# Block norms from channel-major squares, and h of two blocks kept in SBUF

## The chip, the cores and the metric

One core of a Trainium2 chip runs the kernel. The metric is device time in microseconds of one launch, the median of a few runs. The trace is of one further, profiled execution.

## The reference

One layer of a decoder: a pre-norm, one wide input projection, two mixers side by side, one output projection, a post-norm and the residual. What the change touches is the norm, the projection behind it, and the last columns of that projection (`dt_raw`).

```python
def rms_norm(x, w):
    xf = x.astype(jnp.float32)
    y = xf * lax.rsqrt(jnp.mean(xf * xf, axis=-1, keepdims=True) + EPS)
    return (y * w.astype(jnp.float32)).astype(x.dtype)

    h = rms_norm(x, pre_w)                       # x: (1, 2048, 1024)
    proj = jnp.einsum('bld,dc->blc', h, w_in)
    u, v, zg, z, xbc, dt_raw = jnp.split(proj, SPLITS, axis=-1)
    ...
    dt = jax.nn.softplus(dt_raw.astype(f32) + dt_bias.astype(f32))
    ...
    mixed = jnp.einsum('blc,cd->bld', jnp.concatenate([y_a, y_b], axis=-1), w_out)
    return x + rms_norm(mixed, post_w)
```

## The kernel before

The 2048 tokens are four blocks of 512. The 1024 input channels are eight k-tiles of 128, taken as four pairs. `x` comes token-major (`x`) and channel-major (`x_t`).

**Products.** The big projections run as sums of seven products, P1 to P7, of sums and differences of operands, for two pairs of blocks, (0, 2) and (1, 3). Every operand is split into a high and a low part: ScalarE copies (`split`, L160), VectorE subtracts (L161); three wide matmuls of 128x512 follow (`mm3`, L165 to L167, into `acc`). Such a wide matmul is called a wide product below. A step is 24 of them. There are seven units of output columns, 28 steps in each of the first six and 56 in the last. In unit 0, steps 0 to 3 are P1 and P2 of the first pair, which need block 0 alone; steps 4 to 7 are those of the second pair, which need block 1; steps 8 to 11 are P6 and P7 of the first pair (blocks 0 and 2), steps 12 to 15 those of the second (blocks 1 and 3). A product's finished sum is copied out of PSUM by ScalarE (`p` for P1, `stage` for P2). Sums have five PSUM banks.

**`prep(b)`**, once for each block: loads eight tiles of `x` by tokens (`load_x`, L239), squares and sums them on ScalarE (L184), makes `x_ms` (L171, VectorE) and the reciprocal root `x_r` (L173, a power on GpSimd), puts it on a diagonal `dg` (L254, VectorE), and spreads it over partitions on TensorE (`r_ps`, L259; copied to `rb`, L261). It then loads `x_t` in four pieces (L265), scales them in place by the norm's weight and `rb` (L268, eight operations on VectorE), stores them to `hd` in HBM (L269), and computes `dt_ps`, 32 small matmuls of 128x16 on TensorE (L273; each has two records in the trace). `make_a` loads the operands of P1 to P7 from `hd` again (L153).

**Order.** Each engine takes its instructions in a fixed order, and so does SP, which issues nearly all DMAs. `prep` and other side work are tasks that are advanced between wide products; the numbers given to `spawn` and `yield` say how much later a task goes on:

```python
    spawn(prep(0))
    spawn(setup())
    spawn(prep(1), 1)
    spawn(prep(2), 16)
    spawn(prep(3), 30)
```

`setup` loads constants and has one GpSimd product over `wsT` (L129). A load from `w_u` brings weights; `a<-as0P...` (L736) loads a split operand that unit 0 stored, for use in later units. Tiles come from pools: `rt` takes one of 7 (128x1024), `gt` one of 32 (128x512).

Of the kernel before, what the change touches and what calls it, by code (L numbers as in the profile page):

```python
# [15 lines left out]
P = 128  # L16
# [35 lines left out]
def hybrid_kernel(ctx: ExitStack, tc: tile.TileContext, x, x_t, pre_w, w_u, w_o, w_dt,  # L52
# [15 lines left out]
    def bank(name):  # L68
        return ps.tile([P, T], F32, name=name, tag="ps")
# [4 lines left out]
    def gt(name):  # L74
        return gfull(name)[:, 0:T]
# [4 lines left out]
    def rt(name):  # L80
        return rpool.tile([P, 2, T], F32, name=name, tag="r")
# [94 lines left out]
    def rsqrt_mean2(ss, n, inv, name):  # L176
        tot = sm.tile([P, n], F32, name=name + "_tot")
        nc.vector.tensor_tensor(tot, ss[:, :, 0], ss[:, :, 1], ALU.add)
        return rsqrt_mean(tot, n, inv, name)
# [3 lines left out]
    def sumsq(dst, src, n):  # L183
        nc.scalar.activation(junk[:, 0:n], src, AF.Square, accum_out=dst)  # L184
# [17 lines left out]
    def spawn(gen, delay=0):  # L202
        task = [now[0] + delay, gen]
        tasks.append(task)
        if delay == 0:
            advance(task)
        return task
# [24 lines left out]
                then()  # L232


    def load_x(b):
        for c in range(NT):
            for n in range(2):
                xt = gt("xt")
                nc.sync.dma_start(out=xt, in_=x[(b * NT + c) * P:(b * NT + c + 1) * P, n * WC:(n + 1) * WC])  # L239
                yield c, n, xt  # L240

    def prep(b):

        ss = sm.tile([P, NT, 2], F32, name="x_ss")
        dg = gt("dg").rearrange("p (c n) -> p c n", c=NT)
        for c, n, xt in load_x(b):
            sumsq(ss[:, c, n:n + 1], xt, WC)
        if b == 0:
            for i, v in enumerate((dt_bias, a_log, d_skip)):
                nc.sync.dma_start(out=hvec[:, i, :], in_=v.partition_broadcast(P))  # L250
            nc.scalar.activation(na, hvec[:, 1, :], AF.Exp)
            nc.vector.tensor_scalar(na, na, -1.0, None, ALU.mult)
        r = rsqrt_mean2(ss, NT, 1.0 / DM, "x")
        nc.vector.tensor_tensor(dg, ident[:, :].unsqueeze(1).broadcast_to([P, NT, P]),  # L254
                                r[:, :].unsqueeze(2).broadcast_to([P, NT, P]), ALU.mult)
        if b:
            yield 0
        rp = bank("r_ps")
        nc.tensor.matmul(rp, lhsT=ones, rhs=dg.rearrange("p c n -> p (c n)"), start=True, stop=True)  # L259
        rb = gt("rb")  # L260
        nc.vector.tensor_copy(rb, rp)  # L261
        dtp = bank("dt_ps")
        for j in range(4):
            h = rt("h")
            nc.sync.dma_start(out=h, in_=x_t[b, j])  # L265
            for kk in range(2):
                k = 2 * j + kk
                nc.vector.scalar_tensor_tensor(h[:, kk, :], h[:, kk, :], pre_c[:, k:k + 1], rb, ALU.mult, ALU.mult)  # L268
            nc.sync.dma_start(out=hd[b][j], in_=h)  # L269
            for kk in range(2):  # L270
                k = 2 * j + kk
                for c in range(NT):
                    nc.tensor.matmul(dtp[:, c * NH:(c + 1) * NH], lhsT=h[:, kk, c * P:(c + 1) * P], rhs=wdt[:, k, :],  # L273
                                     start=k == 0 and c == 0, stop=k == KT - 1 and c == NT - 1, skip_group_check=True)
            if b:
                yield 0
        d = sm.tile([P, NG, NT, HG], F32, name=f"dt{b}", bufs=1)
        bias = hvec[:, 0, :].rearrange("p (g h) -> p g h", g=NG)
        for c in range(NT):
            nc.vector.tensor_tensor(d[:, :, c, :], dtp[:, c * NH:(c + 1) * NH].rearrange("p (g h) -> p g h", g=NG),  # L280
                                    bias, ALU.add)
        spawn(dt_chain(b, d), 20)
# [429 lines left out]
    def a_piece(u, p, m, k, j):  # L712
        b = PAIRS[p][m]
        if u < 6:
            return hd[b][2 * k + j]
        assert all((b, (0 if k else 4) + j, i) in y_in for i in range(2))
        return y_d[b][(0 if k else 4) + j]
# [3 lines left out]
    def make_a(u, p, name, j):  # L721

        piece = lambda m, k: a_piece(u, p, m, k, j)
        tt = nc.vector.tensor_tensor
        if name in PLAIN_A and not 1 < u < 6:
            t, = load([piece(*PLAIN_A[name])])
            yield
            w = split(apool, "a", t)
            if u == 1:
                store(a_d[p][name, j], w[:, :, :, :].bitcast(F32))  # L730
            yield w
            return
        if 0 < u < 6:
            yield
            w = apool.tile([P, 2, 2, T], F32R, name="a")
            nc.sync.dma_start(out=w[:, :, :, :].bitcast(F32), in_=a_d[p][name, j][:, :, :, :])  # L736
            yield w
            return
        if u == 0:
            yield  # L740
        if name == "P6":
            if u == 0:
                t, q, r = load([piece(0, 0), piece(1, 0), piece(1, 1)])
                tt(t, t, q, ALU.subtract)
                s3_in[p, j] = t
                tt(r, r, t, ALU.subtract)
                s2 = s2_in[p, j] = [gt("s2") for _ in range(2)]
                for kk in range(2):
                    nc.gpsimd.tensor_copy(s2[kk], r[:, kk, :])
                t = r  # L750
            else:
                q, t = load([piece(1, 1), s_d[p, "S3", j]])
                yield
                tt(t, q, t, ALU.subtract)
                store(s_d[p, "S2", j], t)
        elif name == "P7":
            if u == 0:
                t = s3_in.pop((p, j))
            else:
                t, q = load([piece(0, 0), piece(1, 0)])  # L760
                yield
                tt(t, t, q, ALU.subtract)
                store(s_d[p, "S3", j], t)
        elif name == "P5":
            t, q = load([piece(1, 0), piece(1, 1)])
            if u:
                yield
            tt(t, t, q, ALU.add)
        elif u == 0:
            t, = load([piece(0, 1)])  # L770
            s2 = s2_in.pop((p, j))
            for kk in range(2):
                tt(t[:, kk, :], t[:, kk, :], s2[kk], ALU.subtract)
        else:
            t, q = load([piece(0, 1), s_d[p, "S2", j]])
            yield
            tt(t, t, q, ALU.subtract)
        w = split(apool, "a", t)
        if u == 0:
            store(a_d[p][name, j], w[:, :, :, :].bitcast(F32))  # L780
        yield w
# [128 lines left out]

    nc.sync.dma_start(out=pre_c, in_=pre_w)
    nc.sync.dma_start(out=wdt, in_=w_dt)
    spawn(prep(0))
    spawn(setup())
    spawn(prep(1), 1)
    spawn(prep(2), 16)
    spawn(prep(3), 30)

    LAST = 3
    groups = [[i] for i in range(len(steps) - LAST)] + [list(range(len(steps) - LAST, len(steps)))]  # L920
# [86 lines left out]
```

## Time and profile before

| | us |
|---|---|
| median of 3 runs | 1588.78 (1585.33 to 1590.7) |
| the profiled execution | 1584.35 |
| its span | 1582.6 |
| TensorE busy in the span | 1508.9 (95%) |
| VectorE busy | 1068.9 (68%) |
| ScalarE busy | 819.8 (52%) |
| GpSimd busy | 390.1 (25%) |

The span is what the trace covers; the execution has 1.75 us around it. The engines work side by side, so their busy times add up to more than the span. The kernel moves 494.63 MB by DMA. The granted clock of TensorE, averaged over the span, is 0.979 of full speed.

### The profile page before, as it was taken

The page shows a single profiled execution, that of the slowest core. Times are in us where ns is not written, and L with a number is a line of the kernel's source. Part 1 is how long each engine was busy: PE and PEld are TensorE (multiplying, and loading weights), DVE is VectorE, ACT ScalarE, POOL GpSimd, SP SyncE. Part 2 cuts the span into 40 slices and gives each one's busy share as a digit, 9 for nine tenths or more (in the row PEclk, how much of TensorE's full clock was granted, in tenths as well). Part 3 has the DMA queues.
Part 4 walks back from the last instruction along what each step waited for, and adds up shares of the span by engine and source line. Part 5 has one row for each costly group of instructions (what it writes and reads, how often), then busy time and mean ns, then how long its engine had stood idle before and what let it go on. Part 6 is the DMA issues. An engine that isn't in the chain of part 4 may idle for free.

```text
span 1582.6 us, 21521 instructions
## 1 busy us (share of the span) xinstructions
PE 1508.9 (95%) x7268; PEld 1258.4 (80%) x7268; DVE 1068.9 (68%) x1708; ACT 819.8 (52%) x1769; POOL 390.1 (25%) x449
## 2 busy tenths in 40 slices
PE   4979999899999999999999999989999999999996
PEld 3868887788888888888778888867888878888775
DVE  3476874678665576567786768764665646587698
ACT  4432324655676545654466666859737742333332
POOL 1000000234232333342234515353523300000022
PEclk9988999999999999999999999989999999999999
DMA  9799999999998799986998788866776598897998
GB/s 333 264 371 357 338 411 397 392 340 366 374 349 311 240 353 341 329 316 238 333 338 319 271 299 275 279 229 225 276 252 242 193 302 326 275 384 239 341 351 333
DMA packets 160847, 494.63 MB, mean 313 GB/s; under 512 B 19040, under 2 KB 35808, under 8 KB 140768
## 3 DMA queue, kind: packets, MB, share of 16 engines
q1 hardware_dynamic: 160736, 493.25, 85.9%
q8 instruction: 57, 0.93, 0.2%
q14 instruction: 54, 0.44, 0.1%
HBM read 373.51 MB, written 119.67 MB: 312 GB/s over the span
## 4 chain that ended last, share of the span: by engine, by line
PE 57%; DMA 13%; DVE 11%; ACT 7%; issue 3%; POOL 1%; SPq 1%; DVEq 0%; ACTq 0%; POOLq 0%
PE acc L165 16%; PE acc L167 16%; PE acc L166 16%; DMA E<-scr 3%; DMA r<-yd 3%; PE y_ps L448 3%; ACT E L389 2%; DMA r<-w_o 2%; PE y_ps L451 1%; PE st_ps L453 1%; DVE cv_out L372 1%; DVE a L161 1%; PE s_ps L594 1%; PE y_tp L553 1%; DVE b L161 1%
## 5 line engine op out<-in xcount | busy, mean ns | idle before, releaser
L165 PE MATMUL acc<-b,a 128*128 128x512 f32 x1344 | 544.6, 406 | 16.1 <-DMA a<-as0P 5.4
L166 PE MATMUL acc<-b,a 128*128 128x512 f32 x1344 | 527.3, 392 | 0.0
L167 PE MATMUL acc<-b,a 128*128 128x512 f32 x1344 | 520.2, 393 | 4.3 <-DVE a L161 4.3
L165 PEld LDWEIGHTS acc<-b,a 128*128 128x128 f32 x1344 | 253.7, 189 | 71.3 <-DMA a<-as0P 5.6
L167 PEld LDWEIGHTS acc<-b,a 128*128 128x128 f32 x1344 | 253.2, 188 | 60.2 <-DVE a L161 6.3
L166 PEld LDWEIGHTS acc<-b,a 128*128 128x128 f32 x1344 | 254.0, 189 | 49.3
L160 ACT ACTIVATE a<-r 128x1024 fp32r<-128x1024 f32 x96 | 101.1, 1057 | 200.8 <-PE acc L167 88.5
L165 PE MATMUL acc<-a,b 128*128 128x512 f32 x448 | 182.4, 414 | 8.3 <-ACT b L160 4.2
L372 DVE SCALAR_TENSOR_TENSOR cv_out<-cv_raw,cw,cv_out 128x512 f32<-128x512 f32 x192 | 155.1, 810 | 41.5 <-ACT cv_out L370 39.5
L161 DVE TENSOR_TENSOR b<-r,b 128x1024 fp32r<-128x1024 f32 x112 | 141.9, 1270 | 60.6 <-ACT b L160 60.4
L166 PE MATMUL acc<-a,b 128*128 128x512 f32 x448 | 180.3, 403 | 0.8 <-DVE a L161 0.8
L167 PE MATMUL acc<-a,b 128*128 128x512 f32 x448 | 177.7, 400 | 0.0
L160 ACT ACTIVATE b<-r 128x1024 fp32r<-128x1024 f32 x112 | 117.2, 1052 | 86.9 <-PE acc L167 33.1
L161 DVE TENSOR_TENSOR a<-r,a 128x1024 fp32r<-128x1024 f32 x96 | 117.3, 1223 | 50.5 <-ACT a L160 50.3
L165 PEld LDWEIGHTS acc<-a,b 128*128 128x128 f32 x448 | 87.2, 195 | 27.4 <-ACT b L160 4.3
L184 ACT ACTIVATE junk<-y 128x128 bf16<-128x128 f32 (+1 forms) x192 | 65.5, 341 | 83.1 <-POOL y L465 71.4
L457 POOL TENSOR_TENSOR state<-state,ex 128x256 f32<-128x256 f32 x60 | 46.9, 781 | 239.5 <-PE y_ps L451 239.4
L166 PEld LDWEIGHTS acc<-a,b 128*128 128x128 f32 x448 | 86.8, 194 | 19.6 <-DVE a L161 1.8
L167 PEld LDWEIGHTS acc<-a,b 128*128 128x128 f32 x448 | 86.4, 193 | 18.9 <-issue 0.2
L436 POOL TENSOR_TENSOR xde<-xtok,dte 128x256 f32<-128x256 f32 x64 | 52.3, 824 | 165.0 <-ACT xtok L408 158.7
L173 POOL TENSOR_TENSOR o_r<-o_ms,mhalf 128x1 f32<-128x1 f32 x16 | 19.0, 1198 | 295.1 <-DVE o_ms L171 285.0
L389 ACT ACTIVATE E<-E,cs 128x128 f32<-128x128 f32 x256 | 79.6, 390 | 22.2 <-DMA E<-scr 22.2
(163 smaller groups left out, 2125.8 us busy)
## 6 DMA issues: line engine op xcount, KB each, us to landing
a<-as0P SPq DMA_DIRECT2D x64, 1024.0 KB, 7.4
a<-as1P SPq DMA_DIRECT2D x64, 1024.0 KB, 6.2
r<-w_u SPq DMA_DIRECT2D x108, 512.0 KB, 6.4
r<-yd SPq DMA_DIRECT2D x72, 512.0 KB, 5.3
r<-hd SPq DMA_DIRECT2D x48, 512.0 KB, 7.5
r<-w_o SPq DMA_DIRECT2D x36, 512.0 KB, 5.2
E<-scr SPq DMA_DIRECT2D x64, 256.0 KB, 7.4
yd<-yT SPq DMA_DIRECT2D x64, 256.0 KB, 4.4
```

Source lines behind the costliest of these rows:

```text
L160: nc.scalar.activation(w[:, :, 0, :], t, AF.Copy)
L161: nc.vector.tensor_tensor(w[:, :, 1, :], t, w[:, :, 0, :], ALU.subtract)
L165: nc.tensor.matmul(dst, lhsT=a_hi, rhs=b_hi, start=first, stop=False, skip_group_check=True)
L166: nc.tensor.matmul(dst, lhsT=a_hi, rhs=b_lo, start=False, stop=False, skip_group_check=True)
L167: return nc.tensor.matmul(dst, lhsT=a_lo, rhs=b_hi, start=False, stop=last, skip_group_check=True)
L173: nc.gpsimd.tensor_tensor(r, ms, mhalf[:, 0:n], ALU.pow)
L184: nc.scalar.activation(junk[:, 0:n], src, AF.Square, accum_out=dst)
L372: nc.vector.scalar_tensor_tensor(cv, raw[:, j:j + T], cw[:, ti, j:j + 1], cv, ALU.mult, ALU.add)
L389: nc.scalar.activation(E[:, h, :], E[:, h, :], AF.Relu, scale=-1.0, bias=dts[self.b]["cs"][:, o + h:o + h + 1])
L436: nc.gpsimd.tensor_tensor(h4(xde[:, :]), xc, hv(d["dte"], g, c), ALU.mult)
L448: nc.tensor.matmul(yps[:, h * HD:(h + 1) * HD], lhsT=E[:, h, :], rhs=xdt[:, h * HD:(h + 1) * HD], start=True, stop=True)
L457: nc.gpsimd.tensor_tensor(h4(st[:, :]), h4(st[:, :]), ev(d["ex"], 1, g, c), ALU.mult)
```

## The change

`prep` no longer loads `x` by tokens. It loads `x_t` alone, as eight halves of 128x512, and squares those on ScalarE (L257, L260 of the changed kernel). The eight squares are added up by VectorE for block 0, by GpSimd for blocks 1 to 3 (L261). Four TensorE matmuls with a vector of ones (`ss_ps`, L266, 128x2 each) finish the sum over partitions. The rest of the chain is as before (`x_ms`, `x_r`, `dg` L270, `r_ps` L278, `rb` L280). The halves are scaled in place (L285), stored to `hd` by halves (L286), and `dt_ps` is computed from them (L293). The scaled halves of blocks 0 and 1 stay in SBUF (`kept`), and `make_a` splits them from there for P1 and P2 of unit 0 (L754 ScalarE, L755 VectorE) instead of loading from `hd`. The tasks start at other points: `prep(1)` at once, `setup` later, `prep(2)` and `prep(3)` earlier; and a block's `prep` is driven forward when an operand asks for it.

```diff
--- before.py
+++ after.py
@@ -232,45 +232,65 @@
                 then()
 
 
-    def load_x(b):
-        for c in range(NT):
-            for n in range(2):
-                xt = gt("xt")
-                nc.sync.dma_start(out=xt, in_=x[(b * NT + c) * P:(b * NT + c + 1) * P, n * WC:(n + 1) * WC])
-                yield c, n, xt
+    kept, h_in = {}, set()
 
     def prep(b):
 
-        ss = sm.tile([P, NT, 2], F32, name="x_ss")
-        dg = gt("dg").rearrange("p (c n) -> p c n", c=NT)
-        for c, n, xt in load_x(b):
-            sumsq(ss[:, c, n:n + 1], xt, WC)
+
+        xs = []
+        for j in range(4):
+            if b:
+                halves = [gt("x") for _ in range(2)]
+            else:
+                t = rt("x")
+                halves = [t[:, kk, :] for kk in range(2)]
+            for kk in range(2):
+                nc.sync.dma_start(out=halves[kk], in_=x_t[b, j, :, kk, :])
+            xs += halves
         if b == 0:
             for i, v in enumerate((dt_bias, a_log, d_skip)):
                 nc.sync.dma_start(out=hvec[:, i, :], in_=v.partition_broadcast(P))
-            nc.scalar.activation(na, hvec[:, 1, :], AF.Exp)
-            nc.vector.tensor_scalar(na, na, -1.0, None, ALU.mult)
-        r = rsqrt_mean2(ss, NT, 1.0 / DM, "x")
+        else:
+            yield 4
+
+        total = gt("sq")
+        nc.scalar.activation(total, xs[0], AF.Square)
+        for k in range(1, KT):
+            sq = gt("sq")
+            nc.scalar.activation(sq, xs[k], AF.Square)
+            (nc.gpsimd if b else nc.vector).tensor_tensor(total, total, sq, ALU.add)
+        if b:
+            yield 9
+        ssp = bank("ss_ps")
+        for c in range(NT):
+            nc.tensor.matmul(ssp[:, 2 * c:2 * c + 2], lhsT=total[:, c * P:(c + 1) * P], rhs=ones[:, 0:2],
+                             start=True, stop=True)
+        r = rsqrt_mean(ssp[:, 0:2 * NT].rearrange("p (c i) -> p c i", i=2)[:, :, 0], NT, 1.0 / DM, "x")
+        dg = gt("dg").rearrange("p (c n) -> p c n", c=NT)
         nc.vector.tensor_tensor(dg, ident[:, :].unsqueeze(1).broadcast_to([P, NT, P]),
                                 r[:, :].unsqueeze(2).broadcast_to([P, NT, P]), ALU.mult)
         if b:
             yield 0
+        else:
+            nc.scalar.activation(na, hvec[:, 1, :], AF.Exp)
+            nc.vector.tensor_scalar(na, na, -1.0, None, ALU.mult)
         rp = bank("r_ps")
         nc.tensor.matmul(rp, lhsT=ones, rhs=dg.rearrange("p c n -> p (c n)"), start=True, stop=True)
         rb = gt("rb")
         nc.vector.tensor_copy(rb, rp)
         dtp = bank("dt_ps")
         for j in range(4):
-            h = rt("h")
-            nc.sync.dma_start(out=h, in_=x_t[b, j])
             for kk in range(2):
                 k = 2 * j + kk
-                nc.vector.scalar_tensor_tensor(h[:, kk, :], h[:, kk, :], pre_c[:, k:k + 1], rb, ALU.mult, ALU.mult)
-            nc.sync.dma_start(out=hd[b][j], in_=h)
+                nc.vector.scalar_tensor_tensor(xs[k], xs[k], pre_c[:, k:k + 1], rb, ALU.mult, ALU.mult)
+                nc.sync.dma_start(out=hd[b][j][:, kk, :], in_=xs[k])
+            h_in.add((b, j))
+            if b < 2:
+                kept[b, j] = xs[2 * j:2 * j + 2]
             for kk in range(2):
                 k = 2 * j + kk
                 for c in range(NT):
-                    nc.tensor.matmul(dtp[:, c * NH:(c + 1) * NH], lhsT=h[:, kk, c * P:(c + 1) * P], rhs=wdt[:, k, :],
+                    nc.tensor.matmul(dtp[:, c * NH:(c + 1) * NH], lhsT=xs[k][:, c * P:(c + 1) * P], rhs=wdt[:, k, :],
                                      start=k == 0 and c == 0, stop=k == KT - 1 and c == NT - 1, skip_group_check=True)
             if b:
                 yield 0
@@ -712,6 +732,8 @@
     def a_piece(u, p, m, k, j):
         b = PAIRS[p][m]
         if u < 6:
+            while (b, 2 * k + j) not in h_in:
+                advance(preps[b])
             return hd[b][2 * k + j]
         assert all((b, (0 if k else 4) + j, i) in y_in for i in range(2))
         return y_d[b][(0 if k else 4) + j]
@@ -722,6 +744,17 @@
 
         piece = lambda m, k: a_piece(u, p, m, k, j)
         tt = nc.vector.tensor_tensor
+        if u == 0 and name in ("P1", "P2"):
+            yield
+            b, i = PAIRS[p][0], 2 * PLAIN_A[name][1] + j
+            while (b, i) not in kept:
+                advance(preps[b])
+            w = apool.tile([P, 2, 2, T], F32R, name="a")
+            for kk, h in enumerate(kept.pop((b, i))):
+                nc.scalar.activation(w[:, kk, 0, :], h, AF.Copy)
+                nc.vector.tensor_tensor(w[:, kk, 1, :], h, w[:, kk, 0, :], ALU.subtract)
+            yield w
+            return
         if name in PLAIN_A and not 1 < u < 6:
             t, = load([piece(*PLAIN_A[name])])
             yield
@@ -910,11 +943,11 @@
 
     nc.sync.dma_start(out=pre_c, in_=pre_w)
     nc.sync.dma_start(out=wdt, in_=w_dt)
-    spawn(prep(0))
-    spawn(setup())
-    spawn(prep(1), 1)
-    spawn(prep(2), 16)
-    spawn(prep(3), 30)
+    preps = {0: spawn(prep(0))}
+    preps[1] = spawn(prep(1))
+    spawn(setup(), 3)
+    preps[2] = spawn(prep(2), 6)
+    preps[3] = spawn(prep(3), 20)
 
     LAST = 3
     groups = [[i] for i in range(len(steps) - LAST)] + [list(range(len(steps) - LAST, len(steps)))]
```

How the order moves. First VectorE at the program's start, of before (`x_ss`, `x_tot`, `x_ms`, `x_r`: sums of squares up to the reciprocal root; `na`: a small constant):

```order
L103 MEMSET ones 128x128
L105 MEMSET mhalf 128x8
L178 TENSOR_TENSOR x_tot<-x_ss 128x4
L252 TENSOR_SCALAR na<-na 128x16
L171 TENSOR_SCALAR x_ms<-x_tot 128x4
L254 TENSOR_TENSOR dg<-ident,x_r 128x512
L261 COPY rb<-r_ps 128x512
L268 SCALAR_TENSOR_TENSOR h<-h,pre_c,rb 128x512 x8
```

and of the change (`sq`: squares and their sum; `b<-r,b`: the low part of a split weight):

```order
L261 TENSOR_TENSOR sq<-sq 128x512 x6
L276 TENSOR_SCALAR na<-na 128x16
L261 TENSOR_TENSOR sq<-sq 128x512
L161 TENSOR_TENSOR b<-r,b 128x2x512
L171 TENSOR_SCALAR x_ms<-ss_ps 128x4
L161 TENSOR_TENSOR b<-r,b 128x2x512
L270 TENSOR_TENSOR dg<-ident,x_r 128x512
L161 TENSOR_TENSOR b<-r,b 128x2x512
L280 COPY rb<-r_ps 128x512
L285 SCALAR_TENSOR_TENSOR x<-x,pre_c,rb 128x512 x8
```

Three splits of weights now stand between the squares and the scaling of block 0.

Next TensorE where block 1 is prepared. Before, `r_ps` and the `dt_ps` matmuls of block 1 lie in pieces among wide products; this is the first piece of `dt_ps`, eight of the 32:

```order
L165 MATMUL acc<-a,b 128x512
L166 MATMUL acc<-a,b 128x512
L167 MATMUL acc<-a,b 128x512
L273 MATMUL dt_ps<-wdt,h 128x16 x8
L165 MATMUL acc<-a,b 128x512
L166 MATMUL acc<-a,b 128x512
```

In the change this stands behind the 96 wide products of steps 0 to 3:

```order
L165 MATMUL acc<-a,b 128x512
L166 MATMUL acc<-a,b 128x512
L167 MATMUL acc<-a,b 128x512
L266 MATMUL ss_ps<-ones,sq 128x2 x4
L278 MATMUL r_ps<-dg,ones 128x512
L293 MATMUL dt_ps<-wdt,x 128x16 x32
L165 MATMUL acc<-a,b 128x512
```

All of block 1's small work on TensorE has come together in one place, with no wide product inside.

Last SP's queue near the end of unit 0, of before (`t10`, `t11`: sums of weights; `hd2`: scaled x of block 2; numbers behind names tell copies apart):

```order
L230 DMA t11_151<-r_2231 128x1024
L736 DMA a_2344<-as0P61_105 128x2048
L153 DMA r_2630<-t10_150 128x1024
L153 DMA r_2695<-hd2_2_94 128x1024
```

and of the change:

```order
L230 DMA t11_151<-r_2279 128x1024
L153 DMA r_2678<-t10_150 128x1024
L153 DMA r_2743<-hd2_2_94 128x1024
L153 DMA r_2745<-w_u 128x1024
L769 DMA a_2392<-as0P61_105 128x2048
```

The load of `as0P61` stands behind three loads that it stood ahead of. Further on, TensorE's order is the same; ScalarE's has 38 table loads instead of 40, both fewer ones in unit 5.

## Rows read from the trace of the kernel before

**Rows 1.** The page, part 1: busy us, share of the span, instructions.

```profile
PE 1508.9 (95%) x7268; PEld 1258.4 (80%) x7268; DVE 1068.9 (68%) x1708; ACT 819.8 (52%) x1769; POOL 390.1 (25%) x449
```

**Rows 2.** Windows: stretch, length, busy us (instructions) of each engine, PEclk, DMA share, GB/s.

```profile
37.00:155.00 118.00, 108.46 (x501) 90.64 (x502) 72.52 (x141) 42.19 (x77) 5.98 (x8) 0.86 0.89 333
155.00:245.00 90.00, 90.00 (x409) 74.61 (x408) 70.20 (x111) 27.69 (x31) 1.17 (x2) 1.00 0.99 374
245.00:310.00 65.00, 55.89 (x246) 44.98 (x244) 36.45 (x43) 38.15 (x62) 6.03 (x5) 0.95 1.02 393
```

**Rows 3.** Groups, 0 to 155 us, PE: count | busy, mean ns | idle before.

```profile
L165 PE MATMUL acc<-a,b 128*128 128x512 f32 x97 | 43.4, 452 | 7.2 <-ACT b L160 4.2 <-ACT a L160 3.0
...
L259 PE MATMUL r_ps<-dg,ones 128*128 128x512 f32 x8 | 5.2, 741 | 17.9 <-DVE dg L254 17.9
```

**Rows 4.** PE's waits, 250 to 305 us: total, times, longest.

```profile
PE acc L165 <- DMA a<-as0P: 5.2, 1, 5.2
```

**Rows 5.** Timeline, 60 to 70 us, PE: start, duration, operation, idle before.

```profile
61.88 3.64 PE L273 MATMUL dt_ps<-wdt,h 128*128 128x16 f32 x32
...
66.21 0.63 PE L166 MATMUL acc<-a,b 128*128 128x512 f32 x1
66.64 0.63 PE L167 MATMUL acc<-a,b 128*128 128x512 f32 x1
...
69.57 0.39 PE L165 MATMUL acc<-a,b 128*128 128x512 f32 x1
69.80 0.39 PE L166 MATMUL acc<-a,b 128*128 128x512 f32 x1
```

**Rows 6.** Timeline, 0 to 44 us, all engines.

```profile
0.73 1.28 ACT L184 ACT_TABLE_LOAD   x1 [0.73 <-PEq L999]
...
9.11 2.30 SPq L265 DMA_DIRECT2D h<-x_t  x4
...
13.40 1.03 POOL L173 TENSOR_TENSOR x_r<-x_ms,mhalf 128x4 f32<-128x4 f32 x1 [11.74 <-DVE x_ms L171]
...
14.46 0.69 DVE L254 TENSOR_TENSOR dg<-ident,x_r 128x512 f32<-128x512 f32 x1 [1.15 <-POOL x_r L173]
...
17.32 0.69 DVE L261 COPY rb<-r_ps 128x512 f32<-128x512 f32 x1 [2.17 <-PE r_ps L259]
...
18.85 13.83 PE L273 MATMUL dt_ps<-wdt,h 128*128 128x16 f32 x64 [1.57 <-DVE h L268]
19.45 2.88 POOL L129 TENSOR_TENSOR wsT<-wsT,tri 128x1024 f32<-128x1024 f32 x1 [5.03 <-DMA wsT<-ws_t]
...
36.86 0.80 PE L165 MATMUL acc<-a,b 128*128 128x512 f32 x1 [4.18 <-ACT b L160]
...
42.79 0.39 PE L165 MATMUL acc<-a,b 128*128 128x512 f32 x1
```

**Rows 7.** Window of 5 us, columns as in rows 2.

```profile
120.00:125.00 5.00, 5.00 (x25) 4.90 (x25) 4.74 (x6) 3.95 (x6) 1.63 (x2) 0.50 1.01 407
```

**Rows 8.** PE's waits, 60 to 130 us: total, times, longest.

```profile
PE dt_ps L273 <- DVE h L268: 3.0, 1, 3.0
PE acc L165 <- ACT a L160: 3.0, 1, 3.0
PE r_ps L259 <- DVE dg L254: 2.7, 1, 2.7
```

**Rows 9.** DMA issues, 9.0 to 9.4 us: count, KB, us to landing.

```profile
h<-x_t SPq DMA_DIRECT2D x1, 512.0 KB, 4.3
```

**Rows 10.** Groups, 0 to 155 us, VectorE and ScalarE.

```profile
L161 DVE TENSOR_TENSOR b<-r,b 128x1024 fp32r<-128x1024 f32 x8 | 9.7, 1219 | 1.1 <-ACT b L160 1.1
...
L160 ACT ACTIVATE b<-r 128x1024 fp32r<-128x1024 f32 x8 | 8.2, 1054 | 6.4 <-DVE r L800 5.6 <-DMA r<-w_u 0.9
```

**Rows 11.** Groups, whole span, GpSimd.

```profile
L464 POOL TENSOR_TENSOR y<-y,yo 128x256 f32<-128x256 f32 x60 | 49.8, 830 | 53.5 <-DVE yo L463 47.4 <-DMA E<-scr 3.7 <-DMA vd<-stage 1.3
```

**Rows 12.** Tile h on VectorE: duration ns min/median/max.

```profile
L268 DVE SCALAR_TENSOR_TENSOR h<-h,pre_c,rb x32: 652/745/2849, 18.0 to 127.5; 128x512 f32<-128x512 f32 x32
```

## The prediction

> **What bounds the kernel now.** I read the page's totals first, then the windows of the first 310 us (the only part where the change reorders much), then PE's groups, its waits and the timeline there. TensorE is busy 95% of the span [rows 1], so time can be won or lost only where PE idles or its clock is low. From 155 to 245 us PE is busy 90.00 of 90 us [rows 2]; from 37 to 155 it is busy 108.46 of 118, at a mean granted clock of 0.86, and that is where `prep` of blocks 1 to 3 lies. The 97 products of L165 up to 155 us [rows 3] are eight for each of 12 steps, so twelve steps of 24 wide products end there. From 245 to 310 us the DMA share is 1.02 and PE is busy only 55.89 of 65; its largest wait there is 5.2 us for one load `a<-as0P` [rows 2, 4].
>
> The clock has two levels, 2.4 GHz (granted 1.00) and 1.2 (0.50). At the higher PE starts a wide product every 0.23 us, at the lower every 0.43: starts at 66.21 and 66.64 after a burst of small `dt_ps` matmuls, then 69.57 and 69.80 [rows 5]. A `dt_ps` burst is 64 records for a block. At the lower level it takes 13.83 us (block 0, [rows 6]; the clock column reads 1.00 there, but its rate is that of 120 to 125 us, 25 records in 5 us at a granted 0.50, [rows 7]). At the higher level 32 records take 3.64 us [rows 5], a whole block 7.3. So the work from 37 to 155 us is 288 products x 0.23 = 66.2, three bursts 21.9, three `r_ps` 3.9 (5.2 over four blocks, [rows 3]) and some 3 of small sums: 95 of 118. The other 23 us are about 9 of waits (3.0, 3.0 and 2.7 are the large ones, [rows 8]) and 14 of low clock. What the change does to these 23 decides.
>
> **The change part by part.** *Bytes.* Gone are 8 MB of x by tokens and 4 MB of reloads of `hd`, 12 of 494.63 MB. At 333 GB/s [rows 2] this is 36 us of transfer, but none of the waits in rows 8 names a DMA, and PE waits for none from 155 to 245; I value it at nothing by itself. It shows only by removing the 9 us of waits of rows 8, whose cause is a late `x_ms`, `h` or reload; in the sum below these are simply not there.
>
> *Start.* Before: pow at 13.40, `dg` 14.46, `rb` 17.32, `dt_ps` 18.85 to 32.68, then 4.18 us of waiting for the split of the first `w_u` load, first wide product 36.86 [rows 6]. After, `x_t` lands where `x` landed, and the loads of `w_u` follow in the place of `h<-x_t`: issued about 9.11, landed 4.3 later [rows 9], 13.4. In VectorE's order the first split `b<-r,b` now stands ahead of `x_ms`: ScalarE's copy 1.05 to 14.5, the subtraction 1.22 [rows 10] to 15.7, `x_ms` 0.2, pow 1.03 to 17.0 with the second subtraction beside it, `dg` at 17.25: 2.8 later than before. The third subtraction hides under `r_ps`. So `dt_ps` begins at 21.65; 13.8 of burst and four wide products inside it at 0.43 (1.7) bring 37.2. The `w_u` wait has gone, and the same time has come back ahead of it. GpSimd's `wsT` product (2.88) may hold a scaling as it does now, 0 to 1.4 more; I take 0.6: **37.8** against 36.86.
>
> *Steps 0 to 3.* 92 products are left: about 13 at 0.43, 79 at 0.23, 23.8 us: 61.6. Block 1's squares on ScalarE (begun after the first `p` copy, about 46) and seven GpSimd adds are done by then: a GpSimd add of 128x512 is not in the trace. Half of the `wsT` product, which is twice as long, is 1.44; the add `L464`, half as long, averages 830 ns, so 1.7 at most [rows 6, 11]; VectorE's 745 ns for this shape [rows 12] is the floor. I take 1.3, a little under the nearest row, and get about 57. At 1.7 they end near 60: covered, with under 2 us to spare. Behind the eight squares on ScalarE (4.2 at half of L160's 1054 ns each, [rows 10]) stand three `p` copies; PE has five banks for its sums and fills the fifth meanwhile, so I price that wait at nothing, and at 4.2 if the bank doesn't cover it.
>
> *Block 1, now on PE's path in one piece.* The order puts `ss_ps`, `r_ps` and all 32 `dt_ps` matmuls directly behind one another after 96 products, where before they lay in pieces between products. PE then waits through a chain: `ss_ps` (bounded by 0 and the 1.3 of `r_ps`) 0.9, `x_ms` 0.2, pow 1.03, `dg` 0.69, `r_ps` 1.1, `rb` 0.69, one scaling 0.75: 5.4, to 67.0. The burst takes 7.3 or 13.8. I take 13.8: the burst at 120 us came after PE's waits at the granted 0.50, and the one at 61.88, begun from full speed, ended with the clock falling after it [rows 5, 7]; here 5.4 us of near idleness precede it. That gives 80.8. Then come 13 products at the lower rate, as between 36.86 and 42.79, where they still start 0.43 apart [rows 6]: 13 x 0.20 = 2.6 lost.
>
> *Blocks 2 and 3.* Up to step 12: 192 products 44.2, two bursts 14.6, `ss_ps` and `r_ps` 4.0, small sums 2.0, together 64.8. Both bursts now lie whole among the products. What they lose besides: at least 1.6 each (3.4 us at 0.43, as after 61.88), at most 9.1 each (burst at the low level, 6.5, and 2.6 behind it). Bounds 3.2 and 18.2; I take 9.5, a little below the middle, since products stand on both sides of them. Step 12 begins at 80.8 + 2.6 + 64.8 + 9.5 = **157.7** against 155: +2.7.
>
> *After 155.* The order on PE is the same. SP issues `a<-as0P61` behind three loads of 512 KB that it went ahead of before: 1.5 MB at 393 GB/s [rows 2], 0 to 4.0 us in the stretch where a load of its kind is already waited for; I take 1.5. Two table loads of 1.28 us [rows 6] on ScalarE are gone in unit 5: 0 to -2.6, I take -1.3. The first 5.2 us wait for `as0P60` stays: the bytes ahead of it in SP's order are the same; it could shrink to 0 only if the lighter start left the queue ahead. Net +0.2.
>
> **Sum.** +2.7 + 0.2 = +2.9 on the profiled execution's 1584.35 (span 1582.6), 1587.25. That execution lies 4.4 below the median of the runs, 1588.78; the same difference there gives **1591.7**. Under 0.3%, 4.8 us, this kernel's measurement can't tell from no change; this is inside it.
>
> **Rivals.**
> *Slower: the GpSimd sums hold VectorE's scaling.* Block 2's adds are queued on GpSimd right behind block 1's pow, so they run while VectorE scales block 1; the same for block 3's adds and block 2's scaling. The one such overlap in the trace: the `wsT` product ran from 19.45 to 22.33, and one scaling took 2849 ns instead of 745 [rows 6, 12]. If each of the eight scalings waits for an add, a half takes 0.75 + 1.3 = 2.05, and the eight 16.4 us: 2.6 more than the burst at low clock, 9.1 more than at the high. It decides once a half takes over 1.73 us (13.8/8). With block 1 by 2.6 and blocks 2 and 3 at their upper bound (+8.7 on the 9.5) the time is 11.3 above the forecast, **1603**; if only half the adds meet a scaling, 1597. Against it: the adds may be over before, or wait for x. The Trainium skill, "SBUF — State Buffer", section "Who interferes with whom", gives this as a rule: a VectorE instruction with two inputs in SBUF contends with a GpSimd instruction that reads SBUF, and the one that issued second waits until the other ends. The trace agrees by that one scaling of 2849 ns. By the rule every meeting costs an add's length, and the sum would be this rival's.
>
> *Faster: the clock holds.* If block 1's burst runs at the high level (7.3 for 13.8) and loses 1.6 behind it instead of 2.6, the time is 7.5 lower, 1584.2; if blocks 2 and 3 also lose only 3.2, another 6.3 lower, **1578**. For it: the burst at 61.88 kept its rate to the end; with the loads lighter, nothing else is late. Against: PE idles before each.
>
> *No effect.* From 245 to 310 us the loads set the pace. A delay of two or three us at step 12 is swallowed if the loads of that stretch are issued as early as before: 1588.8.
>
> **How the numbers follow.** Forecast 0.45 (its own range 1584 to 1599), slower rival 0.22, faster rival 0.23, no effect 0.10. Faster by over 0.3%: 0.19 of the faster rival and 0.04 of the forecast, 0.23. Slower: 0.20 of the slower rival and 0.15 of the forecast, 0.35. Within: 0.42. The range 1578 to 1603 leaves out the ends of both rivals, under 2 in 10.
>
> **What would show it.** Right: first bulk of wide products near 37.8; `dt_ps` of block 1 as one burst of about 13.8 us beginning near 67; step 12 near 158; `r<-hd` in the first steps gone. The lock shows as `x<-x,pre_c,rb` at over 1.7 us each beside `sq<-sq` on GpSimd. Wrong: block 1's `dt_ps` in about 7 us, the first product before 35 us, or a wait of PE's for squares or for x, which I priced at none; also any change of PE's gaps after 310 us beyond the two table loads.

## The result, and the profile after

| | before | changed |
|---|---|---|
| median, us | 1588.12 (1581.68 to 1593.81, 18 runs) | 1596.12 (1585.53 to 1604.13, 18 runs) |
| profiled execution's span | 1582.6 | 1601.0 |

The ratio is 1.0054, 95% interval 1.0036 to 1.0071: slower, by 8.0 us of the medians and 8.6 by the ratio. The forecast was 1591.7, in a range of 1578 to 1603. The two profiled spans differ by 18.4 us, more than the medians: the profiled execution of before lies low among its runs, that of the changed kernel (1603.06) high among its own. The traces are therefore read by stages, and a size counts for more where the stage takes as long in other runs.

The page of the changed kernel:

```profile
span 1601.0 us, 21566 instructions
...
PE 1526.1 (95%) x7300; PEld 1273.8 (80%) x7300; DVE 1089.1 (68%) x1719; ACT 812.9 (51%) x1743; POOL 415.5 (26%) x470
```

PE has 32 records more than before (32 for `ss_ps`), and is busy 17 us longer [rows 1]. Where they lie shows in the windows that answer to [rows 2]:

```profile
37.00:155.00 118.00, 111.06 (x496) 95.69 (x496) 71.74 (x117) 36.81 (x64) 37.97 (x28) 0.80 0.58 211
155.00:245.00 90.00, 90.00 (x406) 74.82 (x406) 74.70 (x138) 26.63 (x34) 2.34 (x4) 0.98 0.99 382
245.00:310.00 65.00, 58.51 (x263) 47.17 (x262) 35.06 (x42) 32.81 (x49) 4.27 (x5) 1.00 1.01 385
```

From 37 to 155 us the DMA share has fallen from 0.89 to 0.58 and the mean clock from 0.86 to 0.80. None of PE's waits there names a DMA, so the traffic that was taken out was not what this stretch waited for. PE idles 6.9 of the 118 us, 9.5 before: the loss shows as the lower clock, not as more idle time.

The count of weight loads of wide products gives the time at which a step begins (the first load of its 24):

| begin of step | before | changed | difference |
|---|---|---|---|
| 4 | 69.20 | 87.06 | +17.9 |
| 8 | 115.24 | 131.82 | +16.6 |
| 12 | 154.65 | 165.67 | +11.0 |
| 28 | 244.35 | 255.80 | +11.4 |
| 36 | 300.56 | 309.55 | +9.0 |
| 40 | 329.29 | 342.91 | +13.6 |
| 84 | 631.97 | 646.37 | +14.4 |
| 223 | 1565.29 | 1583.24 | +18.0 |

So there are two places of loss: 11 us before step 12, and 4.6 between steps 36 and 40. From 28 to 36 the load-bound stretch gives 2.4 back. The 3.6 us behind step 84 are spread thin.

**The start.** The timeline that answers to [rows 6]:

```profile
8.65 1.68 SPq L153 DMA_DIRECT2D r<-w_u  x3
...
15.03 1.06 ACT L160 ACTIVATE b<-r 128x1024 fp32r<-128x1024 f32 x1 [2.91 <-DMA r<-w_u]
16.12 1.23 DVE L161 TENSOR_TENSOR b<-r,b 128x1024 fp32r<-128x1024 f32 x1 [3.00 <-ACT b L160]
...
17.26 0.15 DVE L171 TENSOR_SCALAR x_ms<-ss_ps 128x4 f32<-128x4 f32 x1
17.41 1.23 DVE L161 TENSOR_TENSOR b<-r,b 128x1024 fp32r<-128x1024 f32 x1
17.50 2.02 POOL L173 TENSOR_TENSOR x_r<-x_ms,mhalf 128x4 f32<-128x4 f32 x1 [15.85 <-DVE x_ms L171]
...
19.50 2.33 POOL L129 TENSOR_TENSOR wsT<-wsT,tri 128x1024 f32<-128x1024 f32 x1
19.55 2.82 DVE L270 TENSOR_TENSOR dg<-ident,x_r 128x512 f32<-128x512 f32 x1 [0.92 <-POOL x_r L173]
...
24.55 0.69 DVE L280 COPY rb<-r_ps 128x512 f32<-128x512 f32 x1 [1.04 <-PE r_ps L278]
...
26.08 3.60 PE L293 MATMUL dt_ps<-wdt,x 128*128 128x16 f32 x16 [1.57 <-DVE x L285]
...
41.46 0.77 PE L166 MATMUL acc<-a,b 128*128 128x512 f32 x1
```

The first `w_u` load lands 6.4 us after its issue, and its copy begins at 15.03. `x_ms` stands behind the first split and comes at 17.26, though `ss_ps` had ended at 15.04. The second split on VectorE (17.41 to 18.64) lies beside the power on GpSimd, which takes 2.02 us instead of 1.03; then the `wsT` product on GpSimd (19.50 to 21.83) lies beside `dg` on VectorE, which takes 2.82 instead of 0.69. The first wide product of the long run starts at 41.46, against 36.86.

**Block 1.** Its matmuls on PE, in the timeline of PE:

```profile
64.96 0.95 PE L266 MATMUL ss_ps<-ones,sq 128*128 128x2 f32 x8
69.05 2.07 PE L278 MATMUL r_ps<-dg,ones 128*128 128x512 f32 x2 [3.14 <-DVE dg L270]
73.49 13.80 PE L293 MATMUL dt_ps<-wdt,x 128*128 128x16 f32 x64 [2.37 <-DVE x L285]
```

`ss_ps` begins at 64.96, `dt_ps` at 73.49: 8.5 us of chain in which no wide product runs, and then 13.80 us of burst, 64 records as in block 0 at the low rate. VectorE beside it:

```profile
67.25 1.74 DVE L270 TENSOR_TENSOR dg<-ident,x_r 128x512 f32<-128x512 f32 x1 [1.14 <-POOL x_r L173]
...
71.96 9.07 DVE L285 SCALAR_TENSOR_TENSOR x<-x,pre_c,rb 128x512 f32<-128x512 f32 x8
...
104.98 11.50 DVE L285 SCALAR_TENSOR_TENSOR x<-x,pre_c,rb 128x512 f32<-128x512 f32 x8
```

`dg` took 1.74 instead of 0.69 and eight scalings 9.07 us (block 1) and 11.50 (block 2) instead of about 5.4. These are means of two kinds. A scaling beside an add on GpSimd takes 1.75 us, one without 0.74:

```profile
73.26 1.75 DVE L285 SCALAR_TENSOR_TENSOR x<-x,pre_c,rb 128x512 f32<-128x512 f32 x1
...
78.97 0.74 DVE L285 SCALAR_TENSOR_TENSOR x<-x,pre_c,rb 128x512 f32<-128x512 f32 x1
```

Four of block 1's eight scalings are held, six of block 2's; held ones start 1.68 us apart. GpSimd's sums, by the tile (min/median/max of one):

```profile
L261 POOL TENSOR_TENSOR sq<-sq x21: 1261/1315/1670, 51.9 to 113.7; 128x512 f32<-128x512 f32 x21
```

**The load.** PE's wait that answers to [rows 4]:

```profile
PE acc L165 <- DMA a<-as0P: 8.3, 2, 4.8
```

There are two waits now: 4.81 us, which ends at 309.55, for `as0P60` (5.2 before), and 3.53, which ends at 320.41, for `as0P61`.

### The profile page after: what moved, and what is told of

It is laid out like the page before. It is cut to its first block, busy times and chain, and to the rows that moved or that the text cites. A ratio compares the mean times of both kernels' runs of the same rounds, so it can differ in the third digit from the quotient of the medians.

```text
span 1601.0 us, 21566 instructions
## 1 busy us (share of the span) xinstructions
PE 1526.1 (95%) x7300; PEld 1273.8 (80%) x7300; DVE 1089.1 (68%) x1719; ACT 812.9 (51%) x1743; POOL 415.5 (26%) x470
## 4 chain that ended last, share of the span: by engine, by line
PE 65%; DMA 14%; DVE 11%; ACT 5%; issue 3%; POOL 1%; SPq 0%; DVEq 0%; ACTq 0%; POOLq 0%
PE acc L165 18%; PE acc L167 17%; PE acc L166 17%; PE y_ps L468 3%; DMA r<-w_u 2%; PE dt_ps L293 2%; DMA r<-yd 2%; DMA r<-w_o 2%; DMA E<-scr 2%; PE y_ps L471 1%; ACT E L409 1%; PE st_ps L473 1%; PE y_tp L573 1%; PE s_ps L614 1%; DVE a L161 1%
## 5 line engine op out<-in xcount | busy, mean ns | idle before, releaser
L160 ACT ACTIVATE a<-r 128x1024 fp32r<-128x1024 f32 x88 | 92.8, 1057 | 196.9 <-PE acc L167 108.6
L161 DVE TENSOR_TENSOR a<-r,a 128x1024 fp32r<-128x1024 f32 x88 | 107.7, 1226 | 33.1 <-ACT a L160 33.1
```

The source lines that it names most:

```text
L160: nc.scalar.activation(w[:, :, 0, :], t, AF.Copy)
L161: nc.vector.tensor_tensor(w[:, :, 1, :], t, w[:, :, 0, :], ALU.subtract)
```

## The experiments

Theory O: the order costs the time. The norm of block 1 stands behind 96 wide products in one piece with its burst, the splits stand ahead of block 0's norm, and `as0P61` stands behind three loads. Theory L, its rival: GpSimd's sums hold VectorE, and this stretches the chain and the scalings.

**e1, sums on VectorE.**

```diff
-            (nc.gpsimd if b else nc.vector).tensor_tensor(total, total, sq, ALU.add)
+            nc.vector.tensor_tensor(total, total, sq, ALU.add)
```

> The changed kernel with one edit: the squares of all four blocks are added up on VectorE, none on GpSimd. Theory O (the order: block 1's chain and its whole dt_ps burst stand in one piece on TensorE, at the low clock) expects little: the burst stays 13.8 us, only dg of block 1 falls from 1.74 to 0.69 us and the first scaling comes sooner, so step 4 begins 1 to 2 us before 87.06 and step 12 1 to 3 before 165.67. Theory L (GpSimd's sums hold VectorE's scaling) expects the scaling of blocks 1 and 2 to fall from 9.07 and 11.50 to 6.0 us, and step 12 to begin 6 to 9 us earlier, at 157 to 160. Against it in both: seven adds of 0.69 us more on VectorE for each block.

Measured: 1589.97 us, ratio to before 1.0000 (0.9979 to 1.0021): under the changed kernel by 6 us of the medians, 8.6 by the ratios. Step 4 begins at 77.45, step 12 at 153.72. All scalings are free of GpSimd (tile `x` on VectorE):

```profile
L285 DVE SCALAR_TENSOR_TENSOR x<-x,pre_c,rb x32: 741/746/752, 22.6 to 135.2; 128x512 f32<-128x512 f32 x32
```

Step 12 begins 12.0 us earlier, more than either theory expected (1 to 3, 6 to 9), but the gain is not where L puts it. From step 4 to step 12 it takes 76.3 us instead of 78.6, 2.3 less, though block 2's scalings took 6 us less. The larger part lies before step 4. 2.7 us of it are an earlier start in this execution: `dg` was not held there. The rest is at block 1 (PE's timeline):

```profile
59.62 0.95 PE L266 MATMUL ss_ps<-ones,sq 128*128 128x2 f32 x8
...
63.50 1.02 PE L278 MATMUL r_ps<-dg,ones 128*128 128x512 f32 x2
66.18 11.50 PE L293 MATMUL dt_ps<-wdt,x 128*128 128x16 f32 x64 [1.66 <-DVE x L285]
```

The sums are ready sooner, and the scheduler put `ss_ps` 13 products further ahead: wide products run between it and `r_ps`. The edit moved the order too, so this run alone doesn't tell O from L.

**e2, the norm earlier.**

```diff
-            yield 4
+            yield 1
...
-            yield 9
+            yield 4
```

> The changed kernel with the two yields of prep shortened (4 to 1 before the squares, 9 to 4 behind the sums), so that ss_ps and r_ps of block 1 stand among the wide products of steps 1 to 3 and only dt_ps stays behind step 3. Theory O expects the 8.5 us of chain ahead of dt_ps to vanish and the burst to run at least partly at the high clock: step 4 begins at 70 to 79 instead of 87.06, step 12 8 to 14 us before 165.67, and the time falls by about as much, to the kernel before or under it. Theory L, with the sums still on GpSimd, expects the scalings to be held as they are now and step 12 to begin at most 4 us earlier.

Measured: 1582.2 us, ratio 0.9954 (0.9938 to 0.9970): 14 under the changed kernel, and under the kernel before. Step 4 begins at 77.41, step 12 at 149.50. PE's timeline:

```profile
48.35 0.95 PE L266 MATMUL ss_ps<-ones,sq 128*128 128x2 f32 x8
...
56.28 1.02 PE L278 MATMUL r_ps<-dg,ones 128*128 128x512 f32 x2
...
63.30 6.01 PE L293 MATMUL dt_ps<-wdt,x 128*128 128x16 f32 x48
...
69.72 1.72 PE L293 MATMUL dt_ps<-wdt,x 128*128 128x16 f32 x8
71.28 1.84 PE L266 MATMUL ss_ps<-ones,sq 128*128 128x2 f32 x8
72.99 1.87 PE L293 MATMUL dt_ps<-wdt,x 128*128 128x16 f32 x8
```

`ss_ps` and `r_ps` stand among products, no wait of PE's is left from 40 to 170 us, and the burst of block 1 runs for the most part near the high rate. From 37 to 155 us PE is busy all but 0.04 us, at a mean clock of 0.87 (0.80 with the change):

```profile
37.00:155.00 118.00, 117.96 (x557) 101.87 (x558) 85.85 (x155) 39.50 (x66) 38.27 (x31) 0.87 0.73 266
```

VectorE's scalings of block 1 were still held (11.08 us for eight), and it hardly mattered. This is what O expects. By L step 12 would come at most 4 us earlier; it came 16 earlier, 1.6 of them by this execution's earlier start (step 1).

**e3, the splits behind the first scaling.**

```diff
+        with tc.issue_after(scaled[0]) if scaled and len(scaled) < 4 else nullcontext():
             nc.vector.tensor_tensor(w[:, :, 1, :], t, w[:, :, 0, :], ALU.subtract)
+        scaled.append(0)
...
+                sc = nc.vector.scalar_tensor_tensor(xs[k], xs[k], pre_c[:, k:k + 1], rb, ALU.mult, ALU.mult)
+                if b == 0 and k == 0:
+                    scaled[:] = [sc.ins]
```

`tc.issue_after(i)` queues what follows behind the instruction `i` on the same engine; here it holds back three splits.

> The changed kernel with the first three weight splits on VectorE queued behind the first scaling of block 0. If the start is late because these splits stand ahead of x_ms and meet the power on GpSimd (theory O for the start), x_ms comes at about 15.2 instead of 17.26, the power takes 1.03 instead of 2.02, dt_ps begins at 22 to 23.5 instead of 26.08, and all steps up to 12 begin 2.5 to 4 us earlier. If the start is late because of the wsT product on GpSimd or because the loads of w_u land later (theory L, or the loads), dt_ps begins within 1 us of 26.08, since wsT then meets another instruction of the chain.

Measured: 1593.11 us, ratio 1.0018 (1.0002 to 1.0034). `dt_ps` of block 0 begins at 20.95 instead of 26.08, step 12 at 161.85, 3.8 earlier. VectorE's timeline:

```profile
14.56 0.16 DVE L175 TENSOR_SCALAR x_ms<-ss_ps 128x4 f32<-128x4 f32 x1 [1.96 <-PE ss_ps L270]
15.87 0.69 DVE L274 TENSOR_TENSOR dg<-ident,x_r 128x512 f32<-128x512 f32 x1 [1.15 <-POOL x_r L177]
...
19.46 6.07 DVE L289 SCALAR_TENSOR_TENSOR x<-x,pre_c,rb 128x512 f32<-128x512 f32 x8
```

The power is back at 1.15 us of waiting and `dg` at 0.69. The gain is above the expected 2.5 to 4 at the start, since `wsT` no longer met `dg`. But executions of other kernels with the unedited order at the start began `dt_ps` at 25.07 (e2), 24.41 (e4), 23.37 (e1) and 23.00 (e8): 1 to 3 of the 5 us are chance. With the edit it begins at 20.95 to 21.38 in four runs (e3, e5, e6, e10), 3.2 us earlier on average than in the five without it. In e1 and e8 the load of `wsT` landed only behind the power (0.2 and 0.3 us of GpSimd's waiting), so that the product met the third split and not `dg`.

**e4, the load of as0P61 ahead.**

```diff
+            with tc.issue_after(as0P61[0]) if as0P61 else nullcontext():
                 nc.sync.dma_start(out=t, in_=src)
...
+            got = nc.sync.dma_start(out=w[:, :, :, :].bitcast(F32), in_=a_d[p][name, j][:, :, :, :])
+            if (u, p, name, j) == (1, 0, "P6", 1):
+                as0P61.append(got.ins)
```

> The changed kernel with one edit on SP's queue: the load of as0P61 stands ahead of the loads from t10, hd2 and w_u, as in the kernel before. Up to step 36 nothing changes. If the queue place is the cause of the second wait for a<-as0P (3.53 us at 320), that wait falls to under 0.5 us and step 40 begins 3.5 to 5 us earlier against step 36, at about 339; the time falls by 3 to 5 us. If the loads are simply late there because the traffic is full, the wait moves to the next load and step 40 gains under 1.5 us.

Measured: 1588.66 us, ratio 0.9995 (0.9974 to 1.0015). From step 36 to step 40 it takes 29.3 us, with the changed kernel 33.4, before 28.7: 4.0 us. The other runs bear out that this is the queue place: the five with this edit need 29.2 to 30.1 us there, the six without it 33.4 to 34.9. The waits in 255 to 365 us:

```profile
PE acc L168 <- DMA a<-as0P: 4.5, 3, 2.6
```

fell by 3.8 in sum. The median fell by 7.5, more than the stage shows. Of the rest, 1.8 us lie ahead of step 4 in the traces and have nothing to do with the edit, and 2.2 between steps 28 and 36, where a run without it is as short (51.2 us in e2, 51.6 in e4).

**e7, without the kept halves.** The branch of `make_a` that takes `kept` is left out; P1 and P2 load from `hd` as before.

```diff
-        if u == 0 and name in ("P1", "P2"):
...
-            yield w
-            return
```

> The changed kernel without the kept halves: P1 and P2 of unit 0 load scaled x from hd again, as before. If keeping them saves a round trip at the start, the bulk of wide products begins 3 to 6 us later than 41.46 (store, load, split: scaled at 26, stored at 33, loaded at 40 to 44), and the time is 1599 to 1602. If it saves only traffic that nobody waits for, the bulk begins within 1 us and the time is 1595 to 1598. Its order differs: 24 products fewer stand ahead of block 1's dt_ps, so step 4 itself may come earlier.

Measured: 1588.84 us, ratio 1.0005 (0.9985 to 1.0025), 7 under the changed kernel: neither alternative. The bulk begins at 39.58, no later. The order did it, as the last sentence warned:

```profile
47.43 0.95 PE L266 MATMUL ss_ps<-ones,sq 128*128 128x2 f32 x8
...
53.77 1.02 PE L278 MATMUL r_ps<-dg,ones 128*128 128x512 f32 x2
...
59.65 8.87 PE L293 MATMUL dt_ps<-wdt,x 128*128 128x16 f32 x64
```

With the reloads, the scheduler sets `ss_ps` of block 1 behind 24 products and its burst before step 3, where it runs in 8.87 us. So the change without its kept halves loses nothing against before. That its norm isn't late is the likely reason; e2 shows this for the kernel with them, and no run shows it apart here.

**e8, dt_ps in a loop of its own.**

```diff
+            if b:
+                yield 0
+        if b:
+            yield 6
+        for j in range(4):
             for kk in range(2):
                 ...
                     nc.tensor.matmul(dtp[:, c * NH:(c + 1) * NH], ...
```

> The changed kernel with dt_ps of blocks 1 to 3 in a loop of its own behind the scalings, handed out in pieces, so that the wide products of step 4 stand directly behind block 1's r_ps. Theory O with the burst as the cost: the 13.8 us at the low clock fall away from the path and come back as pieces of 7.3 in sum, step 12 begins 5 to 9 us before 165.67, and the time falls by as much. If the chain of 8.5 us and the start are the cost and the burst only fills time in which block 1's operands would be late anyway, step 5 begins about 5 us earlier and step 12 at most 3.

Measured: 1598.79 us, ratio 1.0054 (1.0036 to 1.0071): as the changed kernel. Step 4 begins at 69.35, but these are the three largest of PE's waits from 40 to 170 us:

```profile
PE acc L166 <- DVE a L760: 6.6, 1, 6.6
PE r_ps L278 <- DVE dg L270: 3.1, 1, 3.1
PE acc L165 <- ACT a L759: 2.6, 1, 2.6
```

The 6.6 us are for the split of block 1's kept halves: the products were there, their operands weren't. These splits stand on VectorE behind the eight scalings, which GpSimd's adds stretch from 5.4 us to 9.69, so in this order the hold lies on the path too:

```profile
67.65 9.69 DVE L285 SCALAR_TENSOR_TENSOR x<-x,pre_c,rb 128x512 f32<-128x512 f32 x8
```

Step 5 begins 10.1 us earlier and step 12 9.9, more than the second alternative allowed, but block 3's burst now lies behind it, and at step 16 the gain is 2.6, about what this execution's earlier start gave (`dt_ps` of block 0 at 23.00). Block 1's `dt_ps` ran in pieces, mostly at the high rate, and nothing was gained: the burst's low rate is no cost of its own here, it fills time in which operands are late anyway. So the second alternative stands by its reason, though not by its figures, and the part of theory O that named the burst falls. What is left as the cost is the late norm, with the held scalings behind it.

**e10, two edits** (e3 and e4 together), **e5, three edits** (with e2), **e6**, the same with the sums on VectorE, and **e9**, the three edits without the kept halves. Their edits are those shown.

> The changed kernel with the splits behind the first scaling and the load of as0P61 ahead, the norm as late as in the change. If the late norm of block 1 is the largest cost (theory O), the time is 16 us above that of the three edits less what the late norm leaves: 1585 to 1589, step 4 near 82 and step 12 near 162. If the three edits overlap, 1578 to 1584.

> The changed kernel with three edits at once: the norm of blocks 1 to 3 earlier, the weight splits behind block 0's first scaling, the load of as0P61 ahead. If the three causes stand apart, their gains add: dt_ps of block 0 at 21 us, step 4 at 72 to 74 (77.4 with the earlier norm alone), step 12 at 145 to 147, and 4 us more behind step 36: 1574 to 1577 us, 0.7 to 0.9% under the kernel before. If the load-bound stretch at 245 to 310 us swallows what is gained ahead of it, the time is that of the earlier norm alone less at most 4: 1578 to 1582.

> As the kernel with three edits, and all sums on VectorE. Its order on TensorE is nearly the same (ss_ps of block 1 three rows later), so this run shows the price of GpSimd's sums alone. If they hold VectorE's scalings at a price on the path (theory L), the eight scalings of block 1 take 6 us instead of about 11, its dt_ps ends 3 us earlier, and step 12 begins 3 to 6 us before that of the three edits. If the price is covered by the products queued on TensorE (theory O), step 12 lies within 1.5 us, and the adds on VectorE (21 of 0.69, 14.5 us) may cost as much as they save.

> The kernel with three edits, and P1 and P2 of unit 0 load scaled x from hd again. It shows what the kept halves are worth once the order is mended. If they save the round trip at the start, the bulk of wide products begins 2 to 4 us later than with them and the time is 1574 to 1578. If they are worth nothing, the time is within 2 us of 1572.3.

| | median, us | ratio to before | step 4 | step 12 | step 40 |
|---|---|---|---|---|---|
| e10, two edits | 1586.67 | 0.9978 (0.9959 to 0.9997) | 82.21 | 162.38 | 332.99 |
| e5, three edits | 1572.34 | 0.9893 (0.9872 to 0.9914) | 74.53 | 146.06 | 317.33 |
| e6, and sums on VectorE | 1575.58 | 0.9914 (0.9893 to 0.9934) | 73.12 | 145.78 | 317.34 |
| e9, no kept halves | 1581.99 | 0.9946 (0.9924 to 0.9968) | 78.23 | 152.31 | 323.89 |

e10 met its first alternative in the median and in both steps (its trace is of its slowest execution, 1596.18). Against e5, which differs by the earlier norm alone, it is 14.3 us longer, near e2's 13.9: the late norm is the largest of the three causes in either setting. The gains roughly add: by the medians 3.0 (e3), 7.5 (e4) and 13.9 (e2) are 24.4 us under the changed kernel, and the three edits together 23.8; by the ratios 0.36, 0.59 and 1.00% are 1.95, and the three together 1.61, within their intervals. The page of e5:

```profile
span 1567.6 us, 21565 instructions
...
PE 1514.6 (97%) x7300; PEld 1267.2 (81%) x7300; DVE 1089.1 (69%) x1719; ACT 815.1 (52%) x1743; POOL 428.3 (27%) x470
```

PE is busy 97% of its span. Between e5 and e6 the eight scalings of blocks 1 and 2 are these, e5 first:

```profile
54.76 12.51 DVE L292 SCALAR_TENSOR_TENSOR x<-x,pre_c,rb 128x512 f32<-128x512 f32 x8
...
81.24 6.45 DVE L292 SCALAR_TENSOR_TENSOR x<-x,pre_c,rb 128x512 f32<-128x512 f32 x8
```

```profile
54.88 5.39 DVE L292 SCALAR_TENSOR_TENSOR x<-x,pre_c,rb 128x512 f32<-128x512 f32 x8
...
80.00 5.39 DVE L292 SCALAR_TENSOR_TENSOR x<-x,pre_c,rb 128x512 f32<-128x512 f32 x8
```

12.51 and 6.45 against 5.39, and yet steps 12 and 40 begin at the same time within 0.3 us. Once products cover the chain, GpSimd's hold on VectorE costs nothing up to step 40, as O expects; e6's time isn't clearly different from e5's. How much of e1's gain in the late order was the hold and how much the moved `ss_ps` stays open: the scheduler moves `ss_ps` with the length of the sums, and no edit kept it in place.

In e9 the burst of block 0 is followed by a wait for a split weight:

```profile
24.25 13.83 PE L302 MATMUL dt_ps<-wdt,x 128*128 128x16 f32 x64 [2.20 <-DVE x L292]
40.24 0.80 PE L172 MATMUL acc<-a,b 128*128 128x512 f32 x1 [2.16 <-ACT b L165]
```

The bulk begins at 40.24, and in e5 behind the end of the burst at 36.7: 3.5 us, within the expected 2 to 4, but the time missed both alternatives: the kernel with kept halves is faster by 9.7 us of the medians, 8.4 by the ratios. 6.3 us are there by step 12. This isn't the price of the round trip alone, since the order differs in two more places. In e9 GpSimd takes the `wsT` product ahead of the power, and the `dt_ps` of block 0 begins at 24.25 instead of 21.14 (e5):

```profile
15.86 2.34 POOL L129 TENSOR_TENSOR wsT<-wsT,tri 128x1024 f32<-128x1024 f32 x1 [14.21 <-DMA wsT<-ws_t]
...
18.16 1.03 POOL L180 TENSOR_TENSOR x_r<-x_ms,mhalf 128x4 f32<-128x4 f32 x1
```

And ScalarE has 40 table loads again, as before. What the halves save by themselves stays open. In the order of the change the run without them (e7) was the faster one, by the order that came with it.

## Why the prediction came out as it did

The likeliest case was "no change that can be measured"; the time lies 4.4 us above the forecast and 0.5% above before, inside the range, on the side that had a chance of 0.35. The places of loss were named rightly: the start, block 1's chain, the load of `as0P61`. All three were sized too small, and where the forecast had +2.9 us over before, +8.0 came. That the range held it owes to its width of 25 us, set by two rivals of which neither came whole.

- *Start*: forecast 37.8, measured 41.46. Two prices failed. The load's landing was taken as 4.3 us from the load that stood in that place; it took 6.4, so the splits came 1.6 later. And the one meeting with GpSimd was put on a scaling at 0.6. There were two: the power beside a split (+1.0), which the working had put "beside it" at no price, and `dg` beside `wsT` (+2.1). e3 shows these two gone. This execution's start was the latest of five with this order (e3).
- *Steps 0 to 3*: 23.8 forecast, 23.5 measured. The seven adds took 1.36 us each on average (9.55), forecast 1.3; they ended at 61.5, under cover. The `p` copies cost nothing.
- *Block 1's chain*: 5.4 forecast, 8.5 measured. `dg` was held (+1.05), `r_ps` ran at the low clock (2.07 for 1.1), and the first scaling was held (1.38). The burst was 13.80, forecast 13.8.
- *Blocks 2 and 3*: 2.6 + 64.8 + 9.5 = 76.9 forecast from step 4 to step 12, 78.6 measured.
- *Step 12*: +2.7 forecast, +11.0 measured; the chain and the start are 6.8 of the 8.0 missing.
- *as0P61*: 1.5 taken of 0 to 4.0, measured 4.0 in e4. In a stretch with a DMA share of 1.02 the upper bound was the right one, by the row that stood in the working; e5, e6, e9 and e10 repeat it.
- *The bytes*: worth nothing by themselves, as forecast; the DMA share fell, the waits of [rows 8] went, and PE now waits in block 1's chain instead.
- *The table loads*: -1.3 taken. From step 140 to 150, where the loads differ, the changed kernel needs 97.7 us, before 98.0. One pair doesn't measure it: the other eight runs with 38 loads need 93.9 to 97.0, and e6 and e9, which have 40, 98.8 and 97.3. On average that is 2.1 us for two loads, so the term is not refuted.
- *Swallowing from 245 to 310 us*: from step 28 to 36 the changed kernel takes 2.4 us less than before, of a delay of 11.4. e2, which begins step 28 4.7 us earlier than before, takes less still (51.2 us against 53.8), so this isn't a delay swallowed.
- *The slower rival* had its mechanism and its sign: a held scaling takes 1.75 us, over the 1.7 that it named. But it does not wait a whole add more, as the rival's 2.05 for a half had it: held ones start 1.68 us apart, and only four of eight in block 1 were held, so the scalings took 9.07 us and not 16.4 and the burst of 13.8 still decided. From step 4 to 12 e1 without the hold is 2.3 us faster (its order moved too); e6 gains nothing by taking it away. The Trainium skill, "SBUF — State Buffer", section "Who interferes with whom", is borne out by the 2.02 and 2.82 us at the start. Whether a meeting lies on the path decides what it costs.
- *The faster rival* asked for a burst at the high clock; it ran at the low one.

The stages up to step 40 sum to +13.6, the medians differ by 8.0. The profiled execution of before lies 3.8 us under its median, that of the changed kernel 6.9 above, and from one trace each it can't be said in which stages. Some of it lies at the start: in e4, with the same order up to step 36, step 12 begins 9.1 us after that of before, not 11.0. Some lies in the rest of the kernel, which varies by several us between executions (step 84 to 223: 933.3 us before, 936.9 after, 931.9 in e4).

## What to carry over

In this kernel, bound by TensorE, taking traffic away moved the time only through the order that it left behind. Look at which chain now stands in one piece on the in-order engine, and pull its head forward until products cover it. Here two shortened yields, three held-back splits and one load's queue place turned a loss of 0.5% into a gain of 1.1%. When a new order puts operations of VectorE and GpSimd side by side, price each meeting on the chain, the power on GpSimd too; off the chain they cost nothing that e6 shows. A small change of the order far from the edit (one load behind three others) cost 4 us here, half of what the medians differ by.

## Not expected of the hardware

The hold between VectorE and GpSimd works in both directions: a 128x4 power on GpSimd took 2.02 us beside a split, 1.03 without one. The same order of block 0's start gave `dt_ps` at 23.00, 23.37, 24.41, 25.07 and 26.08 us in five executions, as the loads landed earlier or later. And a burst of 64 small matmuls took 13.80 us behind a chain of 8.5 us without wide products, 11.50 behind one of 6.6 with thirteen (e1), 8.87 behind products (e7).
